# Hybrid encoder, two layers on one core: narrow mLSTM products yielded between projections, mLSTM projected first, grouped-attention outputs kept in SBUF, squares summed on VectorE or TensorE

## The chip, the cores and the metric

One core of a Trainium2 chip runs the whole program. The metric is the device time of one execution in microseconds. The kernel before was run three times beside its profile; lower is better.

## The reference, cut to what matters

```python
for l in range(DEPTH):                                   # DEPTH = 2; x is 1 x 1024 x 1024, float32
    h = rms_norm(x, norm_mix[l])
    (ml_q, ml_k, ml_v, ml_o, ml_g, pool_u,
     d_q, d_k, d_v, g_q, g_k, g_v) = jnp.split(h @ w_in[l], splits, axis=-1)
    y_a = mlstm_mixer(ml_q, ml_k, ml_v, ml_o, ml_g, ...)  # 4 heads, chunks, both directions
    y_b = pool_mixer(pool_u, pool_w[l], pool_scale[l])
    y_c = diff_attention(d_q, d_k, d_v, ...)              # 4 heads, two softmaxes each, norm of the output
    y_d = gqa_axial(g_q, g_k, g_v, ...)                   # 4 query heads, 2 key heads, norms and rotary
    x = x + jnp.concatenate([y_a, y_b, y_c, y_d], axis=-1) @ w_out[l]
    x = x + cross_attention(rms_norm(x, norm_cross[l]), rms_norm(mem, norm_mem[l]), ...)  # mem: 256 tokens
    x = x + conv_ffn(rms_norm(x, norm_ffn[l]), w_ffn_in[l], ...)   # gate, conv over 3 tokens, 2816 wide
```

Everything is float32. An rms_norm needs the sum of the squares of x over the 1024 features of each token.

## The kernel before, in words

Activations are kept feature-major: a tile has 128 features as partitions and 1024 tokens. A float32 product is made of three passes over a high and a low part of each operand, so a product of one weight tile is three matmuls for each input tile and half of the tokens. A helper `dense` emits these at L353, L355 and L357, 512 columns wide in the `sc` banks ("wide" matmuls) and 256 wide in the `fl` and `tp` banks. L328 casts a weight tile on ScalarE and L329 makes its low part on VectorE or GpSimd.

A layer runs in these stages. (1) Fifteen projections (`project` calls named K, Q0, Q1, a0, ... in a string), 48 wide matmuls each, the evacuation on VectorE. Between them run generators from three queues: `pump(1)` emits the next piece of queue 0, `pump(0.6, 1)` of queue 1, which holds `ml_gates` and `ml_steps`, that is the mLSTM with its many products of 65 columns (L959, L1009, L1012) in groups; every `yield c` in a generator hands back and books a cost c, so that where the yields stand decides how many narrow products lie in one piece. `ml_project` (L790) writes q, k and o of the mLSTM through buffers named `e`, of which there are 2, and stores them. (2) Grouped attention (GQA): 4 heads, 64 score products in all (L685, L688, 512 columns), maximum L479 on VectorE, exponential L482 on ScalarE, transposes L537 on TensorE, evacuated twice (L541 ScalarE, L542 VectorE) into buffers `s`, of which there are 8, and then products with the values L527, L528, L530. Each output pair takes an `s` buffer and is stored to memory `yd` (L698); it is loaded again later as input of `w_out`. (3) Differential attention: 128 score products L634 and the same chain, with L491, L510, L511 on GpSimd. Beside (2) and (3) a fill queue gives TensorE other work in the one bank `fl`: the keys and the values of the memory for cross attention (`memory_keys`, `memory_values` L1381 to L1388) and the part of the `w_out` product for the first six inputs (`residual` with 256 columns, 504 such matmuls a layer at L353, L355, L357). (4) The last two inputs of `w_out` (K=2), the tail; each of its 8 output tiles is squared (L243) and the squares added up in `rb` on GpSimd (L244), and 8 products of one column with a vector of ones (L254) then give each token's sum. (5) Cross attention with `w_cq`, scores, `w_co`, squares as in (4). (6) The feed-forward network (L1568 to L1735), `w_ffn_in`, `w_ffn_out`; then the sums for the next layer.

A scheduler puts the recorded instructions of all engines into a fixed order for each engine before the program is built, so the order on an engine is known and doesn't depend on how a run goes. Loads and stores issue from SyncE (SP), in its order.

Of the kernel before, what the change touches and what calls it, by code (L numbers as in the profile page):

```python
# [10 lines left out]
F32 = mybir.dt.float32  # L11
# [40 lines left out]
class Net:  # L52
# [179 lines left out]
    def stats_begin(self, n=S):  # L232
        return {"n": n, "acc": None}

    def stats_add(self, st, x, sq=None):

        nc, n = self.nc, st["n"]
        if st["acc"] is None:
            st["acc"] = self.RB if n == S else self.tile(self.pc, [P, n], F32, f"acc{n}")
            nc.scalar.activation(st["acc"], x, AF.Square)  # L240
        else:
            sq = self.z_() if sq is None else sq
            nc.scalar.activation(sq, x, AF.Square)  # L243
            nc.gpsimd.tensor_tensor(out=st["acc"], in0=st["acc"], in1=sq, op=ALU.add)  # L244

    def stats_end(self, st, RB, bank=None):
# [4 lines left out]
        ps = bank()  # L251
        one = self.cons[:, K_ONE : K_ONE + 1]
        for t in range(nt):
# [124 lines left out]
    def finish_x(self, l, c, k, x, st, alloc):  # L378
# [3 lines left out]
        self.stats_add(st, x)  # L382
# [20 lines left out]
    def qk_chain(self, l, r, cols, band, ind, dim, times, cos, sin, x0, sh, sq, out, parts, then):  # L403
# [7 lines left out]
        yield 3  # L411
# [260 lines left out]
    def gqa_head(self, l, h, kh, kl, V, q, ahead):  # L672
        nc = self.nc
        f, hh = divmod(h, 2)
        out = []

        def group(g):
# [14 lines left out]
            def evac(a, b):  # L692
                if g % 2 == 0:
                    out.append(self.s_())
                o = out[-1][:64]
                nc.vector.tensor_tensor(out=o[:, g % 2 * 256 : g % 2 * 256 + 256], in0=a, in1=b, op=ALU.add)
# [84 lines left out]
    def ml_project(self, l, j, H, dst, scale=None, sigmoid=False):  # L781
# [3 lines left out]
        def evac(sl, ps):  # L785
            t = self.e_()
# [142 lines left out]
    def ml_head(self, l, h, g, HT):  # L929
# [25 lines left out]
        for j in range(2):  # L955
            pc = self.ml_()
            for c in range(4):
# [8 lines left out]
            yield 1  # L966
# [5 lines left out]
        for n in range(2):  # L972
# [28 lines left out]
            yield 1.5  # L1001
            for d in range(2):
                po = self.ml_()
                for c in range(4):
# [5 lines left out]
                    if inter:  # L1010
# [3 lines left out]
                        )  # L1014
                ov = po[:, :260].rearrange("p (c e) -> p c e", e=65)
# [14 lines left out]
                yield 1.5  # L1030
# [38 lines left out]
    def mix(self, l, H, st):  # L1069
# [82 lines left out]
        def first():  # L1152
# [4 lines left out]
            lambda f: qk(5 + f, C_GQ, B_GQA, ind2, 64, dk, table(1), self.GQ[f], (0, 1), (None if f else first))  # L1157
        )
        dkf = lambda f: qk(f, C_DK, B_DIFF, ind4, 32, 1.0, table(0), self.KD[f], (0, 0, 1))
        dqf = lambda f: qk(2 + f, C_DQ, B_DIFF, ind4, 32, dq, table(0), self.QD[f], (0, 1, 0))  # L1160
# [4 lines left out]
        for c in 'K Q0 Q1 a0 b0 p0 p1 k0 b1 q0 a1 k1 q1 o0 o1'.split():  # L1165
# [8 lines left out]
        while self.queues[0]:  # L1174
            self.pump(1)
            self.pump(0.6, 1)
# [5 lines left out]
        Y, Y2 = [], []  # L1182

        def mixed(ks):
            for k in ks:
                Y.append(self.load_pair(self.YD[k], self.tr_, nc.gpsimd if k < 7 else None))
                yield 0

        def heads():
            nonlocal nxt  # L1190
            for h in range(4):
                now = nxt
# [9 lines left out]
                for g, (tasks, mix) in enumerate(self.gqa_head(l, h, *now, ahead)):  # L1202
# [48 lines left out]
    def load_pair(self, src, alloc, lo_engine=None, stage=False):  # L1251
# [3 lines left out]
        nc.sync.dma_start(out=x, in_=src)  # L1255
        hi, lo = alloc(F32R), alloc(F32R)
# [25 lines left out]
    def residual(self, wsrc, K, H, xsrc, xdst, done=None, alloc=None, order=range(KT)):  # L1282

        nc = self.nc
        for m in order:
            x = (alloc or self.z_)()
            nc.sync.dma_start(out=x, in_=xsrc[m])
            ps = self.dense_full(self.weights(wsrc(m), K=K), H)
# [6 lines left out]
    def memory_keys(self, l, mem, alloc, lo_engine):  # L1295
# [54 lines left out]
        for h in range(4):  # L1350
# [7 lines left out]
            for f in range(2):  # L1358
                pr = self.e_(F32R).rearrange("p (s n) -> p s n", n=MEM)
# [6 lines left out]
    def memory_values(self, l, mem, lo_engine):  # L1366
        nc, d = self.nc, self.d
        H, r = mem
        for h in range(4):
# [6 lines left out]
            for t in range(2):  # L1376
# [9 lines left out]
                pr = self.e_(F32R).rearrange("p (s n) -> p s n", n=MEM)  # L1386
# [125 lines left out]
    def cross(self, l, H, r):  # L1512
# [7 lines left out]
        O, last, groups, kv = [], [], [], {0: self.cross_kv(0)}  # L1520
# [30 lines left out]
        return O + last  # L1551
# [95 lines left out]
    def ffn_in(self, l, B):  # L1647
# [20 lines left out]
        for f in range(FT):  # L1668
            rests.append(self.ffn_in_tile(l, f, B, pairs, prepare, rest))
# [3 lines left out]
    def ffn_in_tile(self, l, f, B, pairs, prepare, rest):  # L1673
# [3 lines left out]

# [254 lines left out]
```

## Time and profile before

| | us |
|---|---|
| median of three runs | 3503.95 (3497.33 to 3510.3) |
| the profiled execution's own time | 3500.49 |
| its span, first to last instruction | 3498.7 |
| TensorE busy | 3302.9 (94%) |
| VectorE busy | 2102.3 (60%) |
| ScalarE busy | 1439.2 (41%) |
| GpSimd busy | 681.8 (19%) |
| mean granted TensorE clock | 0.957 of 2.4 GHz |

The share of busy time is an average over stages that differ; busy TensorE at the lower of its two clock levels (1.2 GHz) counts as busy too. So a stage is read by its idle time and by its mean granted clock together.

### The profile page before, as it was taken

How to read it: one execution, taken by the hardware profiler on the slowest of the kernel's cores; microseconds unless marked ns; L12 is line 12 of the kernel's file. 1: busy time of each engine (PE TensorE's matmuls, PEld its weight loads, DVE VectorE, ACT ScalarE, POOL GpSimd, SP SyncE). 2: the span in 40 equal slices, each digit the busy share in tenths (PEclk: the TensorE clock that was granted, in tenths of full speed). 3: DMA queues.
4: the chain of work that ended last, by engine and by line, in shares of the span. 5: the costliest groups of instructions: out<-in, count | busy, mean ns of one | idle time of the engine just before them, and what ended most of it. 6: DMA issues, size and time to landing. Idle time of an engine off the chain costs nothing.

```text
span 3498.7 us, 43627 instructions
## 1 busy us (share of the span) xinstructions
PE 3302.9 (94%) x16782; PEld 2762.6 (79%) x16782; DVE 2102.3 (60%) x3266; ACT 1439.2 (41%) x2411; POOL 681.8 (19%) x484
## 2 busy tenths in 40 slices
PE   7999988999999999999999898899898999999999
PEld 7877777987777888778897777789777878887787
DVE  4445667875456777753435356778735577777432
ACT  4222556753444444431323235577535344434211
POOL 2110435842110000000112004467411100000000
PEclk9988889999999999999999888999999999999999
DMA  5343335423242222255543433344214312222654
GB/s 181 98 127 108 108 92 161 146 75 109 84 144 74 85 79 85 79 189 192 179 130 107 136 96 120 102 157 139 105 61 137 122 61 85 78 85 79 203 189 155
DMA packets 156197, 414.57 MB, mean 118 GB/s; under 512 B 31251, under 2 KB 49301, under 8 KB 155989
## 3 DMA queue, kind: packets, MB, share of 16 engines
q1 hardware_dynamic: 136372, 380.32, 33.0%
q10 hardware_dynamic: 19616, 31.46, 2.8%
q8 instruction: 132, 2.16, 0.3%
q14 instruction: 77, 0.62, 0.1%
HBM read 276.19 MB, written 128.19 MB: 116 GB/s over the span
## 4 chain that ended last, share of the span: by engine, by line
PE 77%; DVE 11%; DMA 6%; ACT 3%; issue 3%; POOL 1%; SPq 0%; ACTq 0%; DVEq 0%; POOLq 0%
PE sc L1681 15%; PE sc L353 11%; PE sc L355 11%; PE sc L357 11%; PE tp L1681 6%; DVE smax L479 2%; PE tp L537 2%; DMA raw<-w_ffn_in 1%; DVE s L542 1%; DMA yd<-s 1%; PE sc L634 1%; PE tp L1009 1%; PE tp L276 1%; PE tp L528 1%; PE tp L1012 1%
## 5 line engine op out<-in xcount | busy, mean ns | idle before, releaser
L328 ACT CAST wp<-raw 128x1024 fp32r<-128x1024 f32 (+2 forms) x174 | 165.4, 952 | 579.8 <-PE sc L355 469.0
L353 PE MATMUL sc<-h,wp 128*128 128x512 f32 x1120 | 361.1, 402 | 18.8 <-DVE e L790 9.6
L357 PE MATMUL sc<-h,wp 128*128 128x512 f32 x1120 | 359.5, 401 | 13.0 <-DVE wp L329 13.0
L355 PE MATMUL sc<-h,wp 128*128 128x512 f32 x1120 | 362.4, 402 | 0.0
L1681 PE MATMUL sc<-h,wp 128*128 128x512 f32 x1320 | 338.4, 397 | 10.7 <-DVE t L1691 7.5
L1681 PE MATMUL sc<-t,wp 128*128 128x512 f32 x1320 | 328.3, 394 | 7.3 <-DVE t L1569 4.1
L1681 PEld LDWEIGHTS sc<-h,wp 128*128 128x128 f32 x1320 | 246.8, 190 | 75.7 <-DVE t L1691 20.7
L1681 PEld LDWEIGHTS sc<-t,wp 128*128 128x128 f32 x1320 | 251.2, 191 | 61.3 <-DVE t L1569 4.7
L244 POOL TENSOR_TENSOR rb<-rb,z 128x1024 f32<-128x1024 f32 x34 | 92.2, 2712 | 901.6 <-ACT z L243 833.6
L353 PEld LDWEIGHTS sc<-h,wp 128*128 128x128 f32 x1120 | 212.8, 193 | 67.9 <-DVE e L790 10.0
L357 PEld LDWEIGHTS sc<-h,wp 128*128 128x128 f32 x1120 | 214.9, 193 | 62.6 <-DVE wp L329 15.2
L479 DVE TENSOR_REDUCE smax<-sc 128x1 f32<-128x1024 f32 x192 | 233.3, 1217 | 43.3 <-PE sc L688 24.2
L355 PEld LDWEIGHTS sc<-h,wp 128*128 128x128 f32 x1120 | 215.5, 193 | 48.8 <-issue 3.5
L482 ACT ACTIVATE h<-sc,smax 128x1024 f32<-128x1024 f32 x192 | 214.8, 1120 | 70.6 <-DVE smax L479 51.8
L1568 ACT CAST wp<-s 128x512 fp32r<-128x512 f32 x176 | 109.2, 623 | 318.6 <-PE sc L1681 296.3
L1289 DVE TENSOR_TENSOR z<-sc,z 128x1024 f32<-128x1024 f32 x64 | 78.3, 1223 | 254.5 <-PE sc L357 254.4
L353 PE MATMUL sc<-t,wp 128*128 128x512 f32 x640 | 201.1, 395 | 12.8 <-ACT wp L328 10.0
L542 DVE TENSOR_TENSOR s<-tp,s 128x512 fp32r<-128x512 f32 x256 | 172.9, 683 | 65.4 <-ACT s L541 64.2
L1681 PE MATMUL tp<-h,wp 128*128 128x512 f32 x792 | 202.0, 390 | 2.3 <-ACT wp L1568 2.3
L355 PE MATMUL sc<-t,wp 128*128 128x512 f32 x640 | 200.6, 395 | 2.4 <-DVE t L1258 2.4
L357 PE MATMUL sc<-t,wp 128*128 128x512 f32 x640 | 198.9, 392 | 0.0
L537 PE MATMUL tp<-identr,h 128*128 128x128 f32 x1024 | 183.1, 284 | 15.3 <-DVE s L542 11.7
(426 smaller groups left out, 7215.0 us busy)
## 6 DMA issues: line engine op xcount, KB each, us to landing
raw<-w_ffn_in SPq DMA_DIRECT2D x88, 512.0 KB
xd<-z SPq DMA_DIRECT2D x72, 512.0 KB
z<-xd SPq DMA_DIRECT2D x72, 512.0 KB
gd<-t SPq DMA_DIRECT2D x44, 512.0 KB
z<-gd SPq DMA_DIRECT2D x44, 512.0 KB
raw<-w_ffn_out SPq DMA_DIRECT2D x32, 512.0 KB
raw<-w_fm SPq DMA_DIRECT2D x30, 512.0 KB
raw<-w_ck SPq DMA_DIRECT2D x16, 512.0 KB
```

The costliest lines, as they stand in the source:

```text
L244: nc.gpsimd.tensor_tensor(out=st["acc"], in0=st["acc"], in1=sq, op=ALU.add)
L328: nc.scalar.copy(hi, raw)
L353: nc.tensor.matmul(o, lhsT=hi[:, k, :], rhs=xh[:, f : f + m], start=first, stop=False)
L355: nc.tensor.matmul(o, lhsT=hi[:, k, :], rhs=xl[:, f : f + m], start=False, stop=False)
L357: nc.tensor.matmul(o, lhsT=lo[:, k, :], rhs=xh[:, f : f + m], start=False, stop=last)
L479: nc.vector.tensor_reduce(out=m, in_=sc, axis=AX.X, op=ALU.max, negate=True)
L482: nc.scalar.activation(e, sc, AF.Exp, bias=m, scale=1.0, accum_out=s)
L537: nc.tensor.transpose(tp[:, (2 * j + i) * P : (2 * j + i + 1) * P], w[:, (k + j) * P : (k + j + 1) * P], self.ident)
L542: nc.vector.tensor_tensor(out=el, in0=tp, in1=eh.bitcast(F32), op=ALU.subtract)
L1289: nc.vector.tensor_tensor(out=x, in0=ps, in1=x, op=ALU.add)
L1568: nc.scalar.copy(hi, x)
L1681: mm = lambda a, b, start, stop: nc.tensor.matmul(ps, lhsT=a, rhs=b, start=start, stop=stop, skip_group_check=not first)
```

## The change

What it does, in the order of the diff:

- Sums of squares. With a bank given (after `w_out`), each tile's squares go at once through 8 products of one column into that bank, which adds up over the tiles; nothing is added on another engine. Without a bank the squares are added on VectorE, no longer on GpSimd.
- `head_norm` and the mLSTM generators yield at more places with smaller costs; `pump(0.7, 1)` in place of `pump(0.6, 1)`.
- The projections go in the order a0 b0 K a1 b1 Q0 Q1 p0 p1 o0 k0 q0 o1 k1 q1; the load of the first GQA keys (`first`) hangs on q0, no longer on Q1.
- `ml_project`, `memory_keys` and `memory_values` take their buffers from `s` (8), no longer from `e` (2).
- GQA outputs stay in two `h` tiles `go`; no store to `yd`, no load from it.
- The first weight tile of `w_co` is asked for before the last group of cross attention.
- The feed-forward network's first tile works on its three products in turn over k, with the sum of squares' end (`scales()`) behind them.

```diff
-            nc.gpsimd.tensor_tensor(out=st["acc"], in0=st["acc"], in1=sq, op=ALU.add)
+            nc.vector.tensor_tensor(out=st["acc"], in0=st["acc"], in1=sq, op=ALU.add)
...
+        if st["ps"] is not None:
+            nc.scalar.activation(sq, x, AF.Square)
+            one = self.cons[:, K_ONE : K_ONE + 1]
+            for t in range(n // P):
+                nc.tensor.matmul(
+                    st["ps"][:, t : t + 1], lhsT=sq[:, t * P : (t + 1) * P], rhs=one, start=st["tiles"] == 0, stop=True,
+                    skip_group_check=st["tiles"] > 0,
+                )
+            st["tiles"] += 1
...
-                if g % 2:
-                    nc.sync.dma_start(
-                        out=self.YD[6 + f, hh * 64 : hh * 64 + 64, g // 2 * HF : (g // 2 + 1) * HF], in_=o
-                    )
+                nc.vector.tensor_tensor(out=o[p0 : p0 + 64, g * 256 : (g + 1) * 256], in0=a, in1=b, op=ALU.add)
...
-            t = self.e_()
+            t = self.s_()
...
+                if c == 1:
+                    yield 0.4
...
-            yield 1.5
+            yield 1
...
+                    if c < 3:
+                        yield 0.4
...
-                yield 1.5
+                yield 0.4
...
-        for c in 'K Q0 Q1 a0 b0 p0 p1 k0 b1 q0 a1 k1 q1 o0 o1'.split():
+        for c in 'a0 b0 K a1 b1 Q0 Q1 p0 p1 o0 k0 q0 o1 k1 q1'.split():
...
-            self.pump(0.6, 1)
+            self.pump(0.7, 1)
...
-                Y.append(self.load_pair(self.YD[k], self.tr_, nc.gpsimd if k < 7 else None))
+                if k < 4:
+                    Y.append(self.load_pair(self.YD[k], self.tr_, nc.gpsimd))
+                else:
+                    Y.append(self.pair_of(go[k - 6], self.tr_, nc.gpsimd if k < 7 else None))
...
-                pr = self.e_(F32R).rearrange("p (s n) -> p s n", n=MEM)
+                pr = self.s_(F32R).rearrange("p (s n) -> p s n", n=MEM)
...
+                if part == 1 and n == 6:
+                    first.append(self.weights(self.d["w_co"][l, 0]))
...
+        for k in range(4 if early else 0):
+            for n, ps in early.items():
+                part(n, ps, True, ws[n], k)
+        if early:
+            prepare(3)
+            scales()
...
-            st, H = self.stats_begin(), []
+            st, H = self.stats_begin(bank=self.tp_), []
```

Two places of the order on an engine, first TensorE in the middle of layer 0's differential attention. Before, at the 24th row of score products (`fl` rows are the `w_out` fill, L537 transposes, L527 and L528 the products with the values):

```order
L528 MATMUL tp_5085<-s_5082,h_4167 64x256
L537 MATMUL tp_5140<-identr,h_4882 128x128
L537 MATMUL tp_5140<-identr,h_4823 128x128
L537 MATMUL tp_5140<-identr,h_4882 128x128
L634 MATMUL sc_5161<-h_4637,h_4799 128x512 x2
L353 MATMUL fl_6187<-t_6153,wp_6637 128x256
L355 MATMUL fl_6187<-t_6154,wp_6637 128x256
L357 MATMUL fl_6187<-t_6153,wp_6638 128x256
L353 MATMUL fl_6187<-t_6159,wp_6637 128x256
L355 MATMUL fl_6187<-t_6160,wp_6637 128x256
L357 MATMUL fl_6187<-t_6159,wp_6638 128x256
L353 MATMUL fl_6187<-t_6165,wp_6637 128x256
```

After, between the 24th and the 26th row (the lines have moved: L644 is the score product, L547 the transpose, L537 to L540 the products with the values, L1398 to L1400 the memory's values):

```order
L547 MATMUL tp_5152<-identr,h_5008 128x128
L547 MATMUL tp_5152<-identr,h_4945 128x128
L547 MATMUL tp_5152<-identr,h_5008 128x128
L1398 MATMUL fl_4974<-wp_4982,h_2939 128x256
L1399 MATMUL fl_4974<-wp_4983,h_2939 128x256
L1400 MATMUL fl_4974<-wp_4982,h_2940 128x256
L644 MATMUL sc_5147<-h_4623,h_4785 128x512 x2
L537 MATMUL tp_5071<-s_5131,h_4157 128x256
L538 MATMUL tp_5071<-s_5132,h_4157 64x256 x2
L540 MATMUL tp_5071<-s_5131,h_4157 128x256
L547 MATMUL tp_5196<-identr,h_4945 128x128
L547 MATMUL tp_5196<-identr,h_5008 128x128
```

Where before a run of fill matmuls of the `w_out` product follows the score pair, after has three of the memory's values and then attention alone. The same queue at the end of layer 0's differential attention, from the last score products on. Before:

```order
L634 MATMUL sc_6582<-h_5746,h_6199 128x512 x2
L527 MATMUL tp_6509<-s_6533,h_5749 128x256
L537 MATMUL tp_6587<-identr,h_6392 128x128
L528 MATMUL tp_6509<-s_6534,h_5749 64x256
L537 MATMUL tp_6587<-identr,h_6449 128x128
L527 MATMUL tp_6509<-s_6533,h_5749 128x256
L537 MATMUL tp_6587<-identr,h_6392 128x128
L528 MATMUL tp_6509<-s_6534,h_5749 64x256
L527 MATMUL tp_6509<-s_6566,h_5749 128x256
L537 MATMUL tp_6587<-identr,h_6449 128x128
L353 MATMUL sc_7383<-h_6345,wp_7378 128x512 x2
L355 MATMUL sc_7383<-h_6346,wp_7378 128x512 x2
```

After (L362, L364, L366 are the `w_out` fill):

```order
L644 MATMUL sc_6564<-h_5732,h_6181 128x512 x2
L547 MATMUL tp_6543<-identr,h_6205 128x128
L538 MATMUL tp_6491<-s_6488,h_5735 64x256
L547 MATMUL tp_6543<-identr,h_6264 128x128
L537 MATMUL tp_6491<-s_6487,h_5735 128x256
L547 MATMUL tp_6543<-identr,h_6205 128x128
L538 MATMUL tp_6491<-s_6488,h_5735 64x256
L547 MATMUL tp_6543<-identr,h_6264 128x128
L362 MATMUL fl_6169<-t_6139,wp_6619 128x256
L364 MATMUL fl_6169<-t_6140,wp_6619 128x256
L366 MATMUL fl_6169<-t_6139,wp_6620 128x256
L362 MATMUL fl_6169<-t_6145,wp_6619 128x256
```

Before, the fill is over here; after, runs of it still stand between the last transposes. And SyncE's queue in layer 0 where the keys of the first GQA head are loaded (L659, L661, L667 before; L669, L671, L677 after). Before:

```order
L1078 DMA z_1629<-rope 128x1024
L1078 DMA z_1630<-rope 128x1024
L1302 DMA z_2780<-memT 128x4x256
L659 DMA t_1554<-gkd 64x1x1024 x2
L659 DMA t_1555<-gkd 64x1x1024 x2
L661 DMA t_1560<-gvd 128x1024
L327 DMA raw_2476<-w_fm 128x1024
L426 DMA gqd<-t_876 128x1024
L795 DMA mkd<-e_1917 128x512
L327 DMA raw_2629<-w_fm 128x1024
L667 DMA t_1562<-gqd 128x1x1024
```

After (L1066 and L1070 load a factor for, and store, the finished mLSTM):

```order
L1066 DMA t_2492<-mod 128x512
L336 DMA raw_3693<-w_ck 128x1024
L1066 DMA t_2492<-mod 128x512
L1066 DMA t_2529<-mod 128x512 x2
L1070 DMA yd<-t_2492 128x512 x2
L336 DMA raw_3953<-w_ck 128x1024
L1070 DMA yd<-t_2529 128x512 x2
L669 DMA t_2788<-gkd 64x1x1024 x2
L669 DMA t_2789<-gkd 64x1x1024 x2
L671 DMA t_2794<-gvd 128x1024
L677 DMA t_2796<-gqd 128x1x1024
```

The key loads stood early among the projections' weights (`w_fm`), and now stand behind the stores of the finished mLSTM.

## Rows read from the trace of the kernel before

**Rows 1.** The page's head and engines: busy time, share of the span, instructions.

```profile
span 3498.7 us, 43627 instructions
PE 3302.9 (94%) x16782; PEld 2762.6 (79%) x16782; DVE 2102.3 (60%) x3266; ACT 1439.2 (41%) x2411; POOL 681.8 (19%) x484
```

**Rows 2.** Windows: length; busy PE, PEld, DVE, ACT, POOL (x); PEclk; DMA share; GB/s.

```profile
97.00:350.00 253.00, 241.93 (x1103) 192.34 (x1103) 123.32 (x249) 66.34 (x133) 24.89 (x20) 0.90 0.39 114
350.00:562.00 212.00, 185.61 (x1065) 158.15 (x1064) 136.69 (x271) 115.00 (x218) 86.41 (x64) 0.86 0.34 106
562.00:745.00 183.00, 174.56 (x1325) 162.41 (x1325) 160.29 (x262) 132.23 (x234) 137.29 (x107) 1.00 0.40 133
821.00:1004.00 183.00, 169.37 (x873) 139.27 (x873) 77.39 (x141) 72.44 (x158) 26.85 (x20) 0.95 0.22 75
1073.00:1115.00 42.00, 35.83 (x142) 28.06 (x140) 31.68 (x56) 18.03 (x31) 2.36 (x1) 0.84 0.14 51
2090.00:2290.00 200.00, 173.51 (x1063) 147.80 (x1061) 136.62 (x269) 114.10 (x215) 85.37 (x64) 0.92 0.35 112
```

**Rows 3.** The same view, drain of the attention and `w_out` tail of layer 0.

```profile
745.00:776.00 31.00, 26.04 (x186) 22.07 (x184) 17.06 (x39) 11.84 (x21) 7.09 (x5) 1.00 0.19 68
776.00:821.00 45.00, 36.80 (x140) 28.44 (x138) 36.74 (x27) 21.95 (x27) 21.01 (x7) 0.89 0.65 228
```

**Rows 4.** TensorE's waits: us in total, times, longest us.

```profile
PE tp L527 <- DVE s L542: 21.4, 9, 8.0
PE sc L357 <- DVE wp L329: 13.0, 5, 3.5
PE sc L353 <- ACT wp L328: 10.0, 2, 5.4
PE sc L353 <- DVE e L790: 9.6, 2, 5.4
```

**Rows 5.** Timeline at the longest of them.

```profile
447.50 0.59 ACT L541 CAST s<-tp 128x512 fp32r<-128x512 f32 x1 [10.52 <-DMA yd<-s]
...
448.87 0.58 PE L527 MATMUL tp<-s,t 128*128 128x256 f32 x1 [7.95 <-DVE s L542]
```

**Rows 6.** Line L1009 by windows: TensorE busy and its matmuls in each stretch.

```profile
350.00:562.00 212.00, 10.75 (x48) 7.62 (x48) 0.86 0.34 106
```

**Rows 7.** Timeline: successive 512-column and 256-column matmuls, and a one-column group.

```profile
748.44 0.62 PE L355 MATMUL sc<-h,wp 128*128 128x512 f32 x2
748.90 0.61 PE L357 MATMUL sc<-h,wp 128*128 128x512 f32 x2
...
759.34 0.28 PE L353 MATMUL tp<-t,wp 128*128 128x256 f32 x1
759.46 0.28 PE L355 MATMUL tp<-t,wp 128*128 128x256 f32 x1
...
820.45 1.84 PE L254 MATMUL fl<-cons,rb 128*128 128x1 f32 x16
```

**Rows 8.** Groups by line: busy us, mean ns, idle before.

```profile
L479 DVE TENSOR_REDUCE smax<-sc 128x1 f32<-128x1024 f32 x192 | 233.3, 1217 | 43.3 <-PE sc L688 24.2 <-PE sc L634 17.2
L1278 DVE TENSOR_TENSOR z<-fl,z 128x256 f32<-128x256 f32 x56 | 23.2, 414 | 3.5 <-PE fl L357 3.4
L1289 DVE TENSOR_TENSOR z<-sc,z 128x1024 f32<-128x1024 f32 x64 | 78.3, 1223 | 254.5 <-PE sc L357 254.4
L244 POOL TENSOR_TENSOR rb<-rb,z 128x1024 f32<-128x1024 f32 x34 | 92.2, 2712 | 901.6 <-ACT z L243 833.6 <-issue 67.5
```

**Rows 9.** Timeline: L329 on VectorE without and with L244 beside it on GpSimd.

```profile
26.96 1.21 DVE L329 TENSOR_TENSOR wp<-raw,wp 128x1024 fp32r<-128x1024 f32 x1
29.10 2.62 DVE L329 TENSOR_TENSOR wp<-raw,wp 128x1024 fp32r<-128x1024 f32 x1 [0.93 <-ACT wp L328]
28.28 2.36 POOL L244 TENSOR_TENSOR rb<-rb,t 128x1024 f32<-128x1024 f32 x1 [4.42 <-ACT t L243]
```

**Rows 10.** Windows: a stretch of the differential attention by itself.

```profile
615.00:660.00 45.00, 44.04 (x343) 41.98 (x342) 40.51 (x64) 32.80 (x59) 37.29 (x30) 1.00 0.42 144
```

More of the change, by code (lines that the diff above doesn't have):

```diff
@@ L250, in stats_end @@
         bank = bank or self.fl_
-        ps = bank()
+        ps = st["ps"] if st["ps"] is not None else bank()
         one = self.cons[:, K_ONE : K_ONE + 1]
-        for t in range(nt):
+        for t in range(nt if st["ps"] is None else 0):
             nc.tensor.matmul(ps[:, t : t + 1], lhsT=st["acc"][:, t * P : (t + 1) * P], rhs=one, start=True, stop=True)
@@ L670, in gqa_query, with gqa_head @@
         return q
-    def gqa_head(self, l, h, kh, kl, V, q, ahead):
+    def gqa_head(self, l, o, p0, kh, kl, V, q, ahead):
         nc = self.nc
-        f, hh = divmod(h, 2)
-        out = []
         def group(g):
@@ L1200, in ahead @@
                         nxt = self.diff_keys(l, 0, self.h_), self.diff_query(l, 0, 0, self.h_)
-                for g, (tasks, mix) in enumerate(self.gqa_head(l, h, *now, ahead)):
+                for g, (tasks, mix) in enumerate(self.gqa_head(l, go[h // 2], 64 * (h % 2), *now, ahead)):
                     if (h, g) == (3,0):
@@ L1280, in residual_steps, with residual @@
             nc.sync.dma_start(out=xdst[m], in_=x)
-    def residual(self, wsrc, K, H, xsrc, xdst, done=None, alloc=None, order=range(KT)):
+    def residual(self, wsrc, K, H, xsrc, xdst, done=None, alloc=None, order=range(KT), made=()):
         nc = self.nc
+        made = deque(made)
         for m in order:
@@ L1519, in cross @@
             self.pump(1, 2)
-        O, last, groups, kv = [], [], [], {0: self.cross_kv(0)}
+        O, last, groups, kv, first = [], [], [], {0: self.cross_kv(0)}, []
         def scores(n):
@@ L1550, in cross @@
         self.wide = False
-        return O + last
+        return O + last, first
     def half_pair(self, x, g, b, lo_engine=None):
@@ L1676, in ffn_in_tile, with part, weights @@
         X, Z, Y = xz[:, :HF], xz[:, HF:], self.pv_()
-        def product(n, ps, first):
-            hi, lo = (t.rearrange("p (k m) -> p k m", m=P) for t in pairs.pop((f, n)))
-            for k, (bh, bl) in enumerate(B[n]):
-                mm = lambda a, b, start, stop: nc.tensor.matmul(
-                    ps, lhsT=a, rhs=b, start=start, stop=stop, skip_group_check=not first
-                )
-                mm(hi[:, k], bh, first and k == 0, False)
-                mm(hi[:, k], bl, False, False)
-                mm(lo[:, k], bh, False, k == 3)
-            prepare(1)
+        def part(n, ps, first, w, k):
+            hi, lo = w
+            bh, bl = B[n][k]
+            mm = lambda a, b, start, stop: nc.tensor.matmul(
+                ps, lhsT=a, rhs=b, start=start, stop=stop, skip_group_check=not first
+            )
+            mm(hi[:, k], bh, first and k == 0, False)
+            mm(hi[:, k], bl, False, False)
+            mm(lo[:, k], bh, False, k == 3)
+        def weights(n):
+            return tuple(t.rearrange("p (k m) -> p k m", m=P) for t in pairs.pop((f, n)))
+        def product(n, ps, first):
+            if n in early:
+                return
+            w = weights(n)
+            for k in range(4):
+                part(n, ps, first, w, k)
+            prepare(1)
+        early = {"11": X, "21": Z, "t1": Y} if f == 0 else {}
+        ws = {n: weights(n) for n in early}
+        for k in range(4 if early else 0):
[4 more added lines that the diff above has]
+            scales()
         g, u = self.z_(), self.t_()
@@ L1750, in run @@
             r = self.stats_end(st, None)
-            O = self.cross(l, H, r)
+            O, first = self.cross(l, H, r)
             B = {n: [] for n in self.PRODUCTS}
@@ L1754, in run @@
             self.residual(
-                lambda m: d["w_co"][l, m], KT, O, self.XD, self.XD, done, order=(0, 4, 1, 5, 2, 6, 3, 7)
+                lambda m: d["w_co"][l, m], KT, O, self.XD, self.XD, done, order=(0, 4, 1, 5, 2, 6, 3, 7),
+                made=first,
             )
-            self.stats_end(st, self.RB)
             end()
-            self.ffn_in(l, B)
+            self.ffn_in(l, B, lambda: self.stats_end(st, self.RB))
             last = l == DEPTH - 1
```

40 lines of the change are left out of this document (22 added, 18 removed).

## The prediction

> **What bounds the kernel now.** The page's head comes first [rows 1]: TensorE is busy for 3302.9 of 3498.7 us, so a gain must come out of the 196 us in which it idles, out of time at its lower clock, or out of work taken off it. A busy share can't say which; the windows by stage do [rows 2, 3], read as busy time and granted clock side by side. The feed-forward network isn't shown there, since TensorE has nothing to give in it. Three kinds of stretch have something. The projections are 242 of 253 us busy, at a clock of 0.90. GQA takes 212 and 200 us, with 186 and 174 busy at 0.86 and 0.92, and no engine is full. The differential attention takes 183 us, with TensorE at 175 and a clock of 1.00, and VectorE at 160. Smaller ones are the `w_out` tail, cross attention and the start of the feed-forward network.
>
> The list of waits then names the stalls [rows 4], and the timeline at the longest shows where it begins [rows 5]: ScalarE waits 10.52 us for an `s` buffer that a GQA store to `yd` still reads, VectorE waits for ScalarE, TensorE for VectorE, 7.95 us.
>
> **The change part by part.** For each stage I counted the instructions along the fixed order of each engine and took durations from rows: a wide matmul 0.23 us (two in 0.46), one of 256 columns 0.12 us, eight one-column products, which leave sixteen records, 1.84 us [rows 7]; a maximum 1.22, a residual addition of 256 columns 0.41, an addition of 1024 columns 1.22 on VectorE and 2.7 on GpSimd [rows 8, 9]. Loads below are such sums at full clock for one layer; the two layers have the same order.
>
> *Projections.* In before, part of the mLSTM ran beside GQA: 48 records of L1009 in layer 0's GQA, 10.75 us [rows 6], as many narrow ones again at L1012, the last 37 wide matmuls, and the gates and the finish. At full clock that is 31 us of TensorE. After, all of it stands ahead of the first GQA score: **+31 us** here. The wait for `e` buffers goes, 9.6 us in two [rows 4]: **-4** in layer 0, **-5** in layer 1. The yields hardly spread the narrow products: the order still has groups of 15 of L1009 and L1012 in one piece. Such groups lie where the clock is low, in the projections at 0.90, which is 25 us lost of 253 [rows 2], for 40 of 64 L1009 products. All 64 would lose 40; the longest runs of before (over 40 products) are down to 29, so I take **+10**, between 0 (spreading works) and 20. The loads of the first keys stand behind the mLSTM's stores, some 27 wide matmuls (6 us) ahead of the first score; three loads in a row rarely land in that time when the queue is full. Bounds 0 and 10.5, the wait for a transfer in [rows 5]; I take **+5**. At the kernel's start GpSimd's additions no longer stretch L329 from 1.21 to 2.62 us [rows 9]: **-4**, once, as a few such stretches stand there.
>
> *GQA.* Its loads fall from 154 us of TensorE, 142 of VectorE and 134 of ScalarE to 122, 122 and 118. The stores and the 8 us stall go. Before, the stage took 1.37 times TensorE's load in layer 0 (212 over 154) and 1.30 in layer 1; at these ratios after would take 167 and 158 us. VectorE at the share that it reaches in the best stretch of the differential attention, 40.5 of 45 us [rows 10], would give 122 / 0.90 = 135. The stall and the narrow products, at which the clock fell, are gone, so I take **148**, nearer the middle: -64 in layer 0, -52 in layer 1.
>
> *Differential attention.* In before its fill was the `w_out` product: 504 matmuls of 256 columns stood between the first and the last score. After, 126 do; the fill stays long at the memory's values, whose result now waits for an `s` buffer among those of the attention. So 378 x 0.12 = 45 us leave this stage. TensorE's load falls from 176 to 130, but VectorE's only from 164 to 155 (21 additions of 0.41), and VectorE is 160 of 183 busy in before [rows 2]. It sets the pace next: 183 x 155 / 164 = 174, **-9**. Bounds: 155 (VectorE's work and no more) and 183 (nothing).
>
> *The displaced fill* comes after the last score, between the last transposes. The drain there has 31 us with 26 busy [rows 3], which hides 5. **+40**, between 25 (it hides waits of the tail too) and 45. So the two attentions gain mostly what the projections and the drain pay: that is the core of this forecast.
>
> *Thin TensorE work.* The rows show the clock at 0.86 where TensorE had 154 us of work in 212, and at 1.00 where it had 176 in 183 [rows 2]. After, the differential attention has 130 in 174, a share of 75%, near that of GQA in before. The Trainium skill, "TensorE: Matmul & The Clock Gate", section "A second HAM failure mode: psum-queue depth-cycling", says that frequent small pauses between groups of matmuls can make the clock swing between its two levels; it speaks against emptying this stage. By the row's own full clock the stage is 174 us; by that rule it is the first slower rival below.
>
> *Sums of squares.* After `w_out` there are 64 one-column products a layer in place of 8, 56 more at 1.84 / 8 = 0.23 us: +12.9 us of TensorE. Against it, the waits for L329 (13.0 us in five [rows 4], four of them in the two tails) and the tail's clock of 0.89 (5 us of 45 [rows 3]) go, since VectorE isn't slowed by L244: -12. **+1**; bounds -6 and +12. Elsewhere 28 additions of 1.22 us go to VectorE: 34 us beside TensorE's dense products, where VectorE has time (at L1289 alone, the residual additions of these stages, it waits 254 us for TensorE [rows 8]); if that cover were gone, 17 us a layer would be due.
>
> *Cross attention and feed-forward start.* The first `w_co` weight comes earlier: 10.0 us in two waits [rows 4], and with the clock of 0.95 over 183 us behind them [rows 2] **-8** a layer; bounds -10 and -4. At the feed-forward start 36 of 42 us are busy at 0.84 [rows 2], 13 us to be had; with three products in turn there is half as much again to do before all inputs are there: **-5**, bounds -10 and 0.
>
> *Sum.* Layer 0: 31 - 4 + 10 + 5 - 4 - 64 - 9 + 40 + 1 - 8 - 5 = -7. Layer 1: 31 - 5 + 10 + 5 - 52 - 9 + 40 + 1 - 8 - 5 = +8. Together +1 on the profiled execution's own 3500.5 us, 3501.5; the median of the runs is 3.5 above that execution, so **3505 us**.
>
> **The rivals.** *The attention runs at VectorE's pace and the narrow products are spread well enough (faster).* GQA 135 us, no clock lost to the moved narrow products, the keys on time: 2 x (13 + 10 + 5) = 56 less, 3449 us. For it: in the stretch of [rows 10] all engines are near full together, so the chain does overlap; against it, that stretch had a full TensorE and a full clock. It beats the forecast's band once GQA is under 140 in both layers.
>
> *TensorE drops to its lower clock in the emptied attention (slower).* GQA then keeps its ratios of before, 167 and 158 (+19 and +10), and the differential attention gains nothing (+9 twice): 47 more, 3552 us. It decides when the granted clock of the differential attention falls under 0.9. For it: the clock of before's GQA; against it, the narrow mLSTM products of that stage, which leave it.
>
> *The `s` buffers run out (slower).* The memory's keys and values are now stored out of `s`, in the middle of the attention, as the GQA outputs were. A stall like that of [rows 5] costs 8 us; with four in a layer 64, 3569 us; from two on it decides. Against it: these buffers hold 512 columns and are stored beside few other loads.
>
> *The spreading does nothing*: by the order it nearly doesn't, and the forecast has that in it.
>
> **How the numbers follow.** A measurement of this kernel can tell about 0.5% (17.5 us) from no change. Chances: the forecast 0.36, the faster rival 0.34, the clock 0.18, the buffers 0.12. Of the forecast's 0.36, 0.30 lies within 0.5%, and 0.03 on either side; of the faster rival 0.03 lies within. With a little of the buffers' case within too: faster 0.34, same 0.34, slower 0.32. The forecast's own range, from the bounds of its terms taken as independent, is 3470 to 3540; to leave out no more than 2 in 10 it must reach both sides: 3445 to 3558.
>
> **What would show it.** In the profile after: GQA of 148 us with a clock over 0.9; the differential attention at 174 with VectorE the fullest; some 70 us from its last score to the end of the mixes, where before took 31; no wait for `e`, `yd` or the first `w_co` weight; mLSTM products and lower clock in the projections; a short wait at the first GQA score. The forecast is wrong if the displaced fill hides something that I hold to be free, if the attention doesn't take up the freed TensorE time, or if waits for `s` appear at the memory's results.

## The result, and the profile after

The changed kernel takes 3770.23 us (3766.98 to 3771.49, four runs) against 3504.84: a ratio of 1.0757, interval 1.0736 to 1.0779. It is 265 us slower; 3505 was forecast, and the range ended at 3558. The profiled execution has a span of 3768.4 us, and the page's head answers to [rows 1]:

```profile
span 3768.4 us, 44008 instructions
PE 3430.0 (91%) x17006; PEld 2838.8 (75%) x17006; DVE 2081.0 (55%) x3294; ACT 1437.8 (38%) x2411; POOL 574.2 (15%) x442
```

TensorE is busy 127 us longer and idles 143 us longer; the mean granted clock fell from 0.957 to 0.923. VectorE, ScalarE and GpSimd are busy for no longer than before. So hardly any work was added: the 224 more records of TensorE are those of the 112 added one-column products. If every matmul's time is weighted with the granted clock while it ran, TensorE's busy time is 3175 us before and 3214 after. So 39 of the 127 us are work at full clock, most of it these products, and the other 88 are the same work at the lower clock. The windows by stage say where (length, busy time of PE, PEld, DVE, ACT and POOL, granted clock, DMA share, GB/s), to be laid beside [rows 2, 3]:

```profile
360.00:416.00 56.00, 27.10 (x132) 21.75 (x130) 20.74 (x47) 9.85 (x14) 6.61 (x3) 0.70 0.39 121
416.00:598.00 182.00, 140.74 (x877) 119.46 (x877) 112.18 (x209) 98.79 (x180) 73.16 (x54) 0.86 0.29 94
598.00:812.00 214.00, 168.24 (x949) 133.19 (x947) 159.29 (x248) 130.51 (x237) 132.87 (x103) 0.85 0.26 82
812.00:833.00 21.00, 20.69 (x175) 20.32 (x174) 13.98 (x24) 10.36 (x18) 9.10 (x7) 1.00 0.27 94
833.00:904.00 71.00, 62.72 (x435) 56.16 (x435) 22.48 (x48) 13.50 (x20) 7.25 (x4) 0.98 0.40 137
904.00:945.00 41.00, 41.00 (x211) 36.17 (x210) 18.74 (x30) 14.30 (x16) 0.00 (x0) 0.79 0.58 201
```

In layer 0 the first GQA score comes at 416 us in place of 350 (forecast +38, measured +66); GQA takes 182 in place of 212; the differential attention 214 in place of 183, longer with less work; and from its last score to cross attention it is 133 us in place of 76 (forecast +41, measured +57). Layer 1 has the same pattern: its first GQA score comes 401 us after the start of its token pass in place of 327 (forecast +41, measured +74), then 183 in place of 200, 218 in place of 183, and 129 in place of 76.

The list of waits of TensorE (us, times, longest) has at its head two that [rows 4] doesn't have:

```profile
PE sc L693 <- DMA t<-gqd: 51.9, 2, 26.8
PE fl L362 <- ACT e L1353: 38.7, 2, 19.7
PE sc L644 <- ACT h L492: 32.9, 45, 1.9
PE tp L547 <- POOL h L521: 21.2, 14, 4.4
```

The first is the load of the first GQA keys and queries. SyncE's and TensorE's timelines (start, duration) show it:

```profile
376.98 0.98 SPq L1070 DMA_DIRECT2D yd<-t  x2
378.05 5.08 SPq L669 DMA_DIRECT2D t<-gkd  x4
383.19 7.43 SPq L671 DMA_DIRECT2D t<-gvd  x1
390.66 1.08 SPq L677 DMA_DIRECT2D t<-gqd  x1
...
415.85 1.22 PE L693 MATMUL sc<-t,t 128*128 128x512 f32 x2 [25.06 <-DMA t<-gqd]
```

The loads stand behind the store of the finished mLSTM, are issued over 14 us, and land 24 us after that. The forecast had the place in the queue right and priced it at 5 us. The second wait is put down to L1353; ScalarE's and SyncE's timelines show what ScalarE waited for:

```profile
499.46 1.20 SPq L1267 DMA_DIRECT2D z<-yd  x1
...
518.03 1.04 ACT L1273 CAST t<-z 128x1024 fp32r<-128x1024 f32 x1 [20.00 <-DMA z<-yd]
```

ScalarE's fixed order has the cast of a loaded mLSTM output behind 14 of the 32 exponentials of GQA; before, it was behind 26. The mLSTM is finished earlier now, so the order puts the cast forward, and all of ScalarE stands for the load.

The text ahead of the prediction says that the key loads hung on Q1 before; by the diff (`None if f else first`) it was Q0.

### The profile page after: what moved, and what is told of

It is laid out like the page before. It is cut to its first block, busy times and chain, and to the rows that moved or that the text cites. A ratio compares the mean times of both kernels' runs of the same rounds, so it can differ in the third digit from the quotient of the medians.

```text
span 3768.4 us, 44008 instructions
## 1 busy us (share of the span) xinstructions
PE 3430.0 (91%) x17006; PEld 2838.8 (75%) x17006; DVE 2081.0 (55%) x3294; ACT 1437.8 (38%) x2411; POOL 574.2 (15%) x442
## 5 line engine op out<-in xcount | busy, mean ns | idle before, releaser
L362 PE MATMUL sc<-h,wp 128*128 128x512 f32 x1120 | 367.9, 408 | 15.2 <-DVE z L744 5.6
L366 PE MATMUL sc<-h,wp 128*128 128x512 f32 x1120 | 365.5, 406 | 0.0
L364 PE MATMUL sc<-h,wp 128*128 128x512 f32 x1120 | 363.6, 405 | 0.0
L1700 PE MATMUL sc<-h,wp 128*128 128x512 f32 x1320 | 337.4, 396 | 22.7 <-ACT wp L1587 15.4
L1700 PE MATMUL sc<-t,wp 128*128 128x512 f32 x1320 | 324.3, 391 | 0.4 <-ACT t L1587 0.4
L1700 PEld LDWEIGHTS sc<-h,wp 128*128 128x128 f32 x1320 | 247.1, 190 | 85.4 <-DVE t L1729 17.8
L1700 PEld LDWEIGHTS sc<-t,wp 128*128 128x128 f32 x1320 | 249.0, 189 | 53.2 <-ACT t L1587 1.2
L362 PEld LDWEIGHTS sc<-h,wp 128*128 128x128 f32 x1120 | 217.1, 197 | 64.4 <-DVE z L744 6.7
L366 PEld LDWEIGHTS sc<-h,wp 128*128 128x128 f32 x1120 | 219.9, 197 | 47.7 <-issue 0.2
L364 PEld LDWEIGHTS sc<-h,wp 128*128 128x128 f32 x1120 | 218.8, 196 | 48.7 <-issue 1.2
L547 PE MATMUL tp<-identr,h 128*128 128x128 f32 x1024 | 190.2, 296 | 38.6 <-POOL h L521 21.2
L362 PE MATMUL sc<-t,wp 128*128 128x512 f32 x640 | 200.4, 394 | 7.6 <-ACT wp L337 4.7
L1700 PE MATMUL tp<-h,wp 128*128 128x512 f32 x792 | 202.2, 391 | 0.0
L364 PE MATMUL sc<-t,wp 128*128 128x512 f32 x640 | 200.0, 394 | 2.4 <-DVE t L1274 2.4
L366 PE MATMUL sc<-t,wp 128*128 128x512 f32 x640 | 198.8, 391 | 0.0
L551 ACT CAST s<-tp 128x512 fp32r<-128x512 f32 x256 | 148.4, 587 | 108.5 <-PE tp L547 89.7
```

Source lines behind the costliest of these rows:

```text
L362: nc.tensor.matmul(o, lhsT=hi[:, k, :], rhs=xh[:, f : f + m], start=first, stop=False)
L364: nc.tensor.matmul(o, lhsT=hi[:, k, :], rhs=xl[:, f : f + m], start=False, stop=False)
L366: nc.tensor.matmul(o, lhsT=lo[:, k, :], rhs=xh[:, f : f + m], start=False, stop=last)
L547: nc.tensor.transpose(tp[:, (2 * j + i) * P : (2 * j + i + 1) * P], w[:, (k + j) * P : (k + j + 1) * P], self.ident)
L551: nc.scalar.copy(eh, tp)
L1700: mm = lambda a, b, start, stop: nc.tensor.matmul(ps, lhsT=a, rhs=b, start=start, stop=stop, skip_group_check=not first)
```

## Experiments

Ratios are to the kernel before, measured beside each kernel; a point is a hundredth of its time, 35 us. Stage lengths of these kernels are told from the last score of one attention to the last of the next, and from a layer's token pass to its first GQA score for the projections; so taken, the differential attention has 185 us in both layers before, and 214 and 218 after. Theory one: the memory's results, taken from the eight `s` buffers, starve the fill, and the late keys add to it. Its rival: the moved mLSTM, the outputs on chip or the one-column products make the kernel slow.

**mem_e.** The memory's results through `e` again:

```diff
-                pr = self.s_(F32R).rearrange("p (s n) -> p s n", n=MEM)
+                pr = self.e_(F32R).rearrange("p (s n) -> p s n", n=MEM)
```

> The changed kernel with one thing undone: the results of the memory's keys and values go through the two e buffers again, no longer through the eight s buffers. By the order, the fill is back beside the attention (504 of the w_out fill's matmuls ahead of the last score, as in the kernel before, in place of 126). Theory, the s buffers starve the fill and the emptied attention then runs slowly: some 140 to 170 us less than the changed kernel, about 3615, and a differential attention near 185 us with a clock over 0.95. Rival, the attention is slow for another reason (outputs kept on chip, the moved mLSTM): less than 40 us gained, the stage still over 205 us.

3620.69 us, 1.0373 (1.0353 to 1.0393): 3.8 points back. The differential attention takes 172 us in both layers, at a clock of 0.98. The theory holds. That this is near the 174 of the forecast is luck: the forecast had the stage without its fill, and here all 504 matmuls of the `w_out` fill stand in it, and none of the memory's values, where before had 144 of those. The values run in GQA now, which takes 204 and 205 us in place of 182 and 183.

**first_q0.** The key loads on Q0 again (`(None if f else first)` moved from `dqf` to `gq`).

> The changed kernel with the loads of the first GQA keys hung on Q0 again, as in the kernel before. Theory, these loads stand behind the mLSTM's stores in SyncE's queue, and TensorE idles and then runs at its lower clock for them: 80 to 100 us less, about 3680, the waits of L693 for gqd (51.9 us) gone. Rival, the first scores would wait for something else at the same place (the mLSTM's own end, or memory's keys): under 30 us less.

3723.35 us, 1.0665 (1.0641 to 1.0689): 0.9 points back, some 32 us, between the two and nearer the rival's. The waits for `gqd` are gone and the projections are 36 and 35 us shorter, but GQA is 12 and 13 us longer.

**both.** Both undone.

> The changed kernel with both of these undone. Theory, they are nearly all that makes it slower and add up: about 3520 us, between 3490 and 3550, 0.99 to 1.015 of the kernel before. Rival, the rest of the change (64 one-column products a layer, mLSTM all ahead of GQA, additions on VectorE) costs much by itself: over 3570 us.

3586.59 us, 1.0269 (1.0249 to 1.0289). The rival's time: the two do add up (3.8 and 0.9 points, 4.9 together), but they are not nearly all, and 2.7% remain.

**before_mem_s.** The kernel before with the edit of mem_e the other way round.

> The kernel before with one thing done: the results of the memory's keys and values through the s buffers. By the order, the fill starves as in the changed kernel (126 of 504 ahead of the last score). Theory, that edit alone costs 120 to 160 us: about 3640. Rival, it needs the other edits to hurt: within 30 us of the kernel before.

3658.08 us, 1.0463 (1.0433 to 1.0492). That edit alone costs 163 us, with nothing else of the change, a little more than the theory had. By stage, the differential attention is 40 and 41 us longer, the stretch from its last score to the first score of cross attention 49 and 53, and GQA 18 and 5 shorter.

**before_vals_s.** The same for the memory's values alone.

> The kernel before, with the results of the memory's values alone through the s buffers (the keys' stay in e). By the order the fill starves just as with both. Theory, the values, which are filled in beside the attention's second half, are what starves: 140 to 165 us slower than before, about 3650. Rival, the keys' stores out of s do a good part of it: under 100 us slower.

3669.08 us, 1.0492 (1.0473 to 1.0511), 174 us slower, more than the theory's 165 and no less than with both. It is the values.

What remains in the kernel with both undone was taken apart next.

**gate.** The cast L1273 held back:

```diff
         hi, lo = alloc(F32R), alloc(F32R)
+        if late is not None:
+            nc.vector.tensor_copy(hi[:64, :1], late)
         nc.scalar.copy(hi, x)
```

> The kernel with both undone, and the cast of each loaded mLSTM and pooling output (L1273) held back by a one-column copy out of the third GQA head's first result, so that it stands behind some 24 of 32 exponentials of GQA on ScalarE in place of 14. Theory, ScalarE sits 20 us for that load in its fixed order and stops the attention, once a layer: 35 to 50 us less, about 3545. Rival, the load itself is late for the fill, and the wait only moves: under 15 us less.

3586.18 us, 1.0246 (1.0222 to 1.027): nothing that can be told from no change, as the rival had it. The 20 us wait at that cast is gone, but GQA is only 3 us shorter, since the wait moved. ScalarE now stands for 16.3 us ahead of the cast of a weight, and TensorE 12.6 us ahead of a GQA score, both with no releaser shown:

```profile
505.27 1.05 ACT L337 CAST wp<-raw 128x1024 fp32r<-128x1024 f32 x1 [16.28 <-issue]
```

So the place of that cast isn't all that makes the stop; what GQA would take without a stop, no run shows. The windows of this kernel's GQA show another place:

```profile
387.00:440.00 53.00, 31.33 (x120) 21.02 (x118) 42.18 (x82) 23.70 (x39) 16.17 (x14) 0.62 0.32 119
```

In its first 53 us TensorE has 31 busy at a clock of 0.62, and VectorE is the busiest. Beside the first scores and exponentials these are the norms of k1 and q1, the last two projections in the new order.

**order.** The old string `K Q0 Q1 a0 b0 p0 p1 k0 b1 q0 a1 k1 q1 o0 o1`, the rest as in both.

> The kernel with both undone, and the projections in the string's old order, which ends on o0 and o1. Theory, in the new order the norms and spreads of k1 and q1, narrow products and waits of TensorE for VectorE, fall into the first GQA scores at the lower clock, and the finished mLSTM's early outputs pull the casts of the stall forward; in the old order both go: 40 to 70 us less, about 3530. Rival, the mLSTM's narrow products in the projections cost it, whatever the order: within 20 us of the kernel with both undone.

3554.12 us, 1.0156 (1.0134 to 1.0179): 1.1 points back, 40 us. The theory holds at the lower end of its range, but the gain lies in the projections as much as in GQA (10 and 15 us there, 10 and 9 in GQA, and 8 and 7 lost in the differential attention).

**yields.** The old yields and 0.6, the rest as in both.

> The kernel with both undone, and the generators' yields and the 0.6 of the pump as before the change, in the new order of projections. Theory, the spreading neither gains nor loses: within 15 us of 3587. Rival, the finer yields are what puts narrow products at the lower clock into the projections: 30 us or more less.

3570.16 us, 1.0202 (1.0181 to 1.0223): 0.7 points back, between the two theories. The finer yields, with the 0.7, cost some 23 us; spreading doesn't pay here, and it isn't free.

**local.** Old order and old yields, the rest as in both.

> The kernel before with only the parts of the change that are neither the order of projections nor the yields, the place of the key loads or the memory's buffers: squares on VectorE and in PSUM, GQA outputs kept on chip, the mLSTM's projections through s, the first w_co weight early, the feed-forward start in turn. Theory by the terms of the forecast (wait for e -9, w_co -16, feed-forward start -10, start -4, sums +2, GQA's stall -8 each): 3450 to 3480, faster than before. Rival, the one-column products and the added work of VectorE eat it: 3490 to 3520.

3525.92 us, 1.0075 (1.0051 to 1.0099): slower than before, and 6 us above the rival's range. The forecast's small gains aren't to be had together.

**local_dve.** Without the bank for the squares after `w_out`:

```diff
-            st, H = self.stats_begin(bank=self.tp_), []
+            st, H = self.stats_begin(), []
```

> The local kernel with the squares after w_out added on VectorE as elsewhere, so 8 one-column products a layer in place of 64. Theory, the one-column products lie on the path of the w_out tail, where the clock then falls, and cost 9 us a layer: 15 to 20 us less than the local kernel, about 3508. Rival, VectorE's eight additions a layer in that tail cost as much: within 5 us.

3494.24 us, 0.9995 (0.9983 to 1.0007): 0.8 points, 28 us, more than the theory had. All of it lies between the attention's last score and the first score of cross attention: 136 us in both layers of the local kernel, 121 and 124 here. The tail in that stretch with the 64 one-column products (the local kernel):

```profile
779.00:826.00 47.00, 44.20 (x214) 36.71 (x213) 27.33 (x30) 22.46 (x27) 0.00 (x0) 0.82 0.64 223
```

and without them:

```profile
780.00:825.00 45.00, 40.65 (x168) 29.75 (x167) 36.03 (x39) 23.43 (x29) 0.00 (x0) 0.96 0.74 260
```

The clock in these windows is 0.82 with them and 0.96 without. GpSimd is idle in both. The windows themselves differ by 2 us only: with the one-column products in between, fewer of the other matmuls come within them.

**local_dve_e.** `ml_project` through `e` as well.

> That kernel with ml_project through the two e buffers again, as before. Theory, the s buffers only turned a wait for e (9.6 us) into one for the loads of the stored keys (23.8 us at L947): 5 to 15 us less, about 3498. Rival, the wait at L947 has another cause, and the wait for e comes back on top: 5 to 10 us more.

3492.62 us, 0.9987 (0.9975 to 1.0): no difference that can be told, so neither. In the local kernel the wait for `e` was gone, and another stood in the list:

```profile
PE tp L947 <- DMA t<-mkd: 23.8, 2, 13.6
```

Here that one is down to 4.1 us, and the wait for `e` is back with 11.5: the one was exchanged for the other, as the theory said, but it isn't worth anything.

**local_dve_e_nogo.** GQA outputs through `yd` again, too.

> That kernel with the GQA outputs stored and loaded again, as before; what is left of the change is the squares added on VectorE, the first w_co weight early and the feed-forward start in turn. Theory, these three gain about 20 us over the kernel before (w_co 8 a layer, start 7 once), and keeping the outputs on chip costs more in the differential attention than it saves: 3475 to 3490. Rival, keeping them saves the 8 us stall a layer: slower than the kernel above by 10 us or more.

3474.55 us, 0.9932 (0.9913 to 0.995), the fastest here: 20 us under the kernel before. Keeping the outputs on chip costs some 19 us. The theory holds in sign and size; its reason only in part: the differential attention gained 7 us in all, layer 0's GQA 17. What each of the three remaining edits gains, no run shows: against the kernel before, layer 0's GQA alone is 17 us shorter and layer 1's 9 longer, and none of the three lies there.

Last, the emptied differential attention is longer with less work on every engine. Theory A: its clock (0.85) makes TensorE's steps of the attention slow. Theory B: the engines wait for each other in the fixed order.

**pad_vals_s.** before_vals_s with idle TensorE work in that stage:

```diff
             tp = self.tp_()
+            for _ in range(pad):
+                nc.tensor.matmul(tp, lhsT=self.identr, rhs=self.mltab[:, :HF], start=True, stop=True)
```

> The kernel before with the memory's values through s (3669 us), and three idle products of 512 columns on TensorE ahead of each group of four transposes of the differential attention, 64 groups a layer, 44 us of TensorE at full clock: work that gives nothing, in place of the missing fill. Their results are overwritten. Theory A, the emptied stage is slow because TensorE's clock falls and its steps of the chain take twice as long: the stage falls from 223 to 185 or 195 us with a clock over 0.95, the whole to 3590 to 3610, in spite of the added work. Theory B, the stage is slow because of its waits in the fixed order: the added work lies in those waits or comes on top, the stage stays at 220 to 260 us.

3690.69 us, 1.0561 (1.0536 to 1.0587): not shorter, 230 and 231 us in place of 223 and 226. The middle of the stage without the idle products:

```profile
620.00:700.00 80.00, 60.21 (x362) 48.95 (x363) 52.72 (x78) 47.80 (x84) 52.74 (x38) 0.91 0.33 101
```

and with them:

```profile
620.00:700.00 80.00, 70.72 (x440) 58.67 (x439) 55.38 (x84) 51.29 (x90) 57.89 (x42) 0.98 0.30 91
```

The clock rose to 0.98 here, and over the whole stage from 0.85 to 0.92 (0.84 to 0.89 in layer 1), so that the clock of over 0.95 that theory A asks for wasn't reached. 44 us of idle work a layer made the stage only 7 and 5 us longer (and what follows it up to cross attention 10 and 11). Each matmul counted to the start of the next, the idle products took 43 us of layer 0's stage, TensorE's other work 149 in place of 171, and its idle time 38 in place of 51. So the higher clock gave 22 us back, and the idle products, which stand in TensorE's order ahead of the transposes, took up that and more. Theory A's forecast failed, but this run doesn't rule out its cause.

**pad_before.** The same in the kernel before.

> The kernel before with the same idle products, as a control. The stage is full there: by either theory it becomes some 40 us longer a layer, 220 to 230 us, the whole 3570 to 3590.

3569.51 us, 1.0208 (1.0184 to 1.0232). The full stage, with TensorE busy for 177 of 185 us already, became 27 and 33 us longer, less than the 40 forecast, but several times the lengthening of the emptied one.

Theory B has a sign in TensorE's order. Transposes issued by the time that a number of score products had been issued (GQA's 64 among them, L685 and L688 counted as one):

```
score products               140  150  160  170  180
transposes, before           380  400  419  440  452
transposes, before_vals_s    376  408  432  434  452
```

Before, they alternate evenly in this stretch. With the values in `s` there are 32 transposes for ten products, then 24, then 2; in the rest of the stage the counts of the two kernels differ by 9 at most. The attention's own split transposes need `s` buffers too, which may be what bunches them; no run shows that step by itself. The time is lost in the same stretch. Score products 140 to 160 take 57 us with the values in `s` (layer 0) and 27 before, which is 30 of the 38 us that the stage is longer; products 160 to 180 take 26 in both. Before, with the values in `s`, and with the idle products as well:

```profile
672.00:699.00 27.00, 26.29 (x207) 25.03 (x206) 23.14 (x38) 19.07 (x34) 22.00 (x19) 1.00 0.48 169
671.00:729.00 58.00, 41.63 (x225) 34.07 (x225) 30.28 (x54) 26.32 (x47) 24.84 (x20) 0.79 0.21 64
679.00:735.00 56.00, 43.95 (x249) 35.45 (x248) 30.71 (x52) 24.73 (x44) 25.26 (x19) 0.88 0.21 66
```

VectorE, ScalarE and GpSimd are busy for 30, 26 and 25 of the 58 us, where they were for 23, 19 and 22 of 27 before: the engines wait for each other. The idle products raised the clock there from 0.79 to 0.88 and left the stretch at 56 us. In the changed kernel these products take 55 us in layer 0. TensorE's waits for the exponential in the stage are 18.2 us after and 1.4 before, and those for L521 9.4. So it is shown where the stage grows, and that the order is uneven there; that the order alone makes it grow is argued, since no run changed the order and left the fill in place.

## Why the prediction was wrong, point by point

By stage, taken between the instructions named, in us a layer (layer 0, layer 1), the changed kernel differs from the kernel before by:

| stage | forecast | measured |
|---|---|---|
| end of the token pass to the first GQA score | +42, +41 | +73, +74 |
| to the last GQA score | -64, -52 | -27, -16 |
| to the last score of the differential attention | -9, -9 | +29, +34 |
| to the first score of cross attention | +41, +41 | +59, +59 |
| to the last product of `w_ffn_in` | -13, -13 | -1, -8 |

*The displaced fill* was seen and was the right place. The step that failed first is the differential attention's: "It sets the pace next" (VectorE), 174 us, -9. The forecast priced the starving as a move of 45 us and left the attention itself unhurt. The stage took 172 where the fill stood beside it (mem_e) and 214 and 218 where it didn't, most of the growth in one stretch of waits. The move itself was priced at 40, with 45 as the upper bound, and is 49 and 53 in before_mem_s. The whole edit costs 163 us by itself on the kernel before and gives 3.8 points back on the changed one. The third rival named these buffers, but as stalls at stores of 8 us each; what they did shows in the order, which is fixed before the run, and where the bunched transposes could have been read as the 126 were.

*The clock rival* was right on the sign that it named (0.85, under 0.9) and too small: it had the stage gain nothing, and the stage lost 29 and 34 us. Whether the clock is a cause of that or goes with the waits stays open: TensorE idles 46 us of this stage in place of 9, and idle products that raised the clock to 0.92 didn't shorten it. The Trainium skill ("TensorE: Matmul & The Clock Gate", section "A second HAM failure mode: psum-queue depth-cycling") says that frequent small pauses between groups of matmuls can make the clock swing between its two levels. The trace agrees in so far as the clock of this stage fell from 1.00 to 0.85 as its idle time grew.

*The keys* were priced at 5 us, with 10.5 as the upper bound, from one transfer's wait. The wait alone was 25.1 us in layer 0; the loads of that place are issued over 14 us and land 24 us later. first_q0 gives 0.9 points back, 32 us, less than the 52 us of its two waits, since GQA takes some of it.

*The moved mLSTM.* The projections were sized right: without the late keys they were forecast 37 and 36 us longer, and with the loads on Q0 again they are 37 and 39. What failed is the other side, GQA at 148. It takes 182 and 183 us in the changed kernel, and TensorE stands 18.9 and 19.7 us of that still for ScalarE's late load, a wait that the forecast didn't have. In the kernel with both undone it takes 218 and 217, 8 and 18 more than before, but there its work isn't less either: with the mLSTM gone, all 192 matmuls of the memory's values run in it, where 48 did before, and TensorE has 1067 records in the stage, before 1051. Nor was the mLSTM what held the clock of this stage down: in before, its own matmuls there ran at a mean granted clock of 0.92 and 0.96, above the stage's 0.86 and 0.92. The end of the new string puts two norms at the start of GQA, at a clock of 0.62 in that stretch. The order and the finer yields together cost 1.9 points (both against local), where the forecast had a gain in GQA to pay for them.

*The squares.* The term was +1 a layer, bounds -6 and +12. From the attention's last score to cross attention the local kernel is 9 us a layer longer than before, inside the bounds; with the sum on VectorE it is 6 and 4 us shorter than before, so the one-column products cost 15 and 13 us against that. Their 12.9 us of TensorE measured 14 a layer in the local kernel. The term also counted on the tail's clock coming back: it does with the sum on VectorE (0.96), and doesn't with the one-column products (0.82, and 0.79 in the changed kernel).

*Small gains.* Wait for `e`: gone in the changed kernel; in the local kernel one for `mkd` took its place. First `w_co` weight and feed-forward start: from cross attention's start to the last product of `w_ffn_in`, 1 and 8 us less than before, where -13 a layer was forecast; a new wait of 7.7 us stands at L1700, for ScalarE's cast of the first weights. Outputs on chip: a loss of 19 us, not the gain of a stall. Start of the kernel: 8 us less up to the end of the token pass, where -4 was forecast.

*Sums.* Some of the working is off by 1 us, and it changes nothing above: 183 x 155 / 164 is 173, not 174; GQA at the old ratio of 212 to 154 would be 168, not 167, and 122 / 0.90 is 136; of 42 us with 36 busy at a clock of 0.84, 12 were to be had.

The parts, in points of the time before, as the pairs of runs give them: memory's buffers 3.8 (changed against mem_e), keys 1.0 (mem_e against both), order and yields 1.9, one-column products 0.8, outputs on chip 0.6, `ml_project` 0.1, and what is left -0.7. These are the steps of one chain from the changed kernel to the kernel before, so they add up to the whole by construction. In another order they differ: the memory's buffers alone cost 4.6 points on the kernel before. Left open is what GQA would take without its late loads, and how much of the emptied attention's growth is its uneven order and how much its clock.

## What to carry to other kernels

Where a scheduler fixes the order, a buffer pool is a part of the order: moving a background result into the pool that the foreground uses held up the background here (126 of 504 matmuls in time), and the foreground's own order was uneven. Compare, before a run, how much of the background stands between the foreground's steps, and whether the foreground's own steps still alternate.

A stage's time isn't given by its fullest engine when the order in it changes: VectorE was busy for 160 us in 183 before and for 159 in 214 after. And work that leaves a stage may make room for other work: count what the new order puts there.

Price added one-column products with the clock of the stretch in which they lie, and a load with all that is issued ahead of it in its queue.

## What the runs showed of the hardware that was not expected

A load of `yd` behind others in SyncE's queue was used 19 us after its issue (499.46 to 518.03), and the issue of a single load (`gvd`) held that queue for 7.43 us, where the same load took 4.68 and 4.90 us in the kernel before. Idle products raised the granted clock of the middle of a stage from 0.91 to 0.98, and the stage was 7 us longer.
